# Differential and latent attention of layer 0 emitted side by side

## The chip, the cores and the metric

One Trainium2 chip, one core. The metric is device time of one execution in microseconds; lower is better. All data are float32; TensorE (PE) multiplies mostly in the float32r format, and a value that needs more precision is carried as a pair "hi" (rounded) and "lo" (the rest).

## What is computed

A trunk of two layers on x (1024 tokens by 1024). Layer 0 has two groups of attention heads beside each other: eight heads of latent attention ("DSA": each query sees the 256 keys that an indexer picked, as a mask here) and four differential heads (two softmax maps each). Their outputs are concatenated and go through one output projection. Cut to layer 0:

```python
def dsa_attention(...):      # 8 heads of 64; s = q_lat.c * scale + bias over the selected keys
    p = softmax(s); return p @ c_sel @ w_uv
def diff_attention(...):     # 4 heads, two maps of 64 each, values of 128
    p = softmax(q.k * scale + bias, causal in chunks of 64)      # (head, map)
    a = p[:, :, 0] - lam * p[:, :, 1]
    return rms_norm(a @ v, b_subln) * (1.0 - lam_init)
def even_mixer(...):
    return concatenate([o_a, o_b], -1) @ w_out
x = x + rms_norm(y, g[1])    # then memory cross-attention, MLP; layer 1 alike with windowed attention
```

## The kernel before

The program is written once, unrolled, in `Net`. `even` (L355) is layer 0's mixer: input projections and the indexer; `topk_steps`, which turns the tile `score` into the tile `mask` with scratch tiles `tk_gt`, `tk_eq`, `tk_w`; the attention; `out_proj`.

Attention works in blocks of 128 queries (eight per head) against all earlier keys. `diff_unit` (L698) is one block of a differential head; `dsa_unit` (L779) one block of a latent head. A unit has steps: `load` (first unit of a head only: a bias tile `H` of 512 KB, the query and key tiles `att_q`, `att_kh`, `att_kl` of 512 KB each per map by `load_qk`, the values `v` of 512 KB, all issued on SP); `probs` (scores on PE into a PSUM bank of tag S, L312 and for the mask L315; bias and row maximum on VectorE (DVE), L329; exponential on ScalarE (ACT), L331; normalising or joining the two maps on GpSimd (POOL)); `flip` (128x128 transposes on PE into a bank of tag T, L255, and copies or hi/lo splits out of it); `pv` (probabilities times values, L743 for differential, L812 for latent heads, one for two blocks); for differential heads also `norm`, `scale`, `back`.

`pipeline` (L40) emits the steps with lags [2, 1, 1, 1, 1, 1]: in L400 all 32 differential units come first and then all 64 latent ones. Emission order is a priority, not the final order: the framework simulates the program with its own times for instructions and transfers, and each engine gets a fixed order out of that simulation, which it then runs strictly in order, waiting on semaphores. PSUM has four banks of tag S and four of tag T.

SBUF is laid out as a stack: pools lie one behind the other in the order in which they are opened (L395 to L399), in the space that the stage before left, and a tile may be written once the old tiles under it have had their last reader. Per partition, behind `mask`, the stage before has `score` at 0 to 16.5 KB, `tk_gt` at 71 to 73, `tk_eq` at 73 to 75 and `tk_w` at 75 to 79 KB, and from 88 KB on the weight tiles (from the other end of SBUF). The attention of before puts six score tiles `s` at 0 to 24 KB, the two `H` at 24 to 32, and, after a filler `gap`, `att_q` from 88 KB on.

Head outputs are stored as hi/lo pairs in `oT` (L773, L774 for differential heads; L817 through `split`, L129 and L130, for latent ones, out of a tile `os`); `out_proj` (L855) uses them as they are. Its eight weights come by `load_w` (L113): a raw tile (two of them), hi on ACT (L120), lo on DVE (L122) or POOL (L125).

Of the kernel before, what the change touches and what calls it, by code (L numbers as in the profile page):

```python
# [12 lines left out]
F32 = mybir.dt.float32  # L13
# [55 lines left out]
class Net:  # L69
# [222 lines left out]
    def load_bias(self, h, pool):  # L292
        nc = self.nc
        H = pool.tile([P, 1024], F32, name="H", bufs=2)
# [23 lines left out]

    def softmax_raw(self, Q, K, H, i, sp, bufs, mask=None):
# [12 lines left out]
        return s, sm  # L332

    def pt_tiles(self, w, pool):
        nc = self.nc
        nk = 2 * w + 2
        out = []
        for c in range((nk + 3) // 4):
            out.append((pool.tile([P, 4, 256], F32R, name="pt_hi", bufs=3),
                        pool.tile([P, 4, 256], F32R, name="pt_lo", bufs=3)))  # L340
# [14 lines left out]
    def even(self):  # L355
        nc, A = self.nc, self.A
        z = {}
        with ExitStack() as sp_:
            with ExitStack() as st:
# [44 lines left out]
            act = self.out_proj(oT, W, A["ev_out"], 1, 2, self.x_in, x1)  # L404
        return act, x1

# [239 lines left out]
    def load_qk(self, zq, zk, j, pool):  # L646
        nc = self.nc
        rows = slice(64 * j, 64 * j + 64)
        q = pool.tile([P, S], F32R, name="att_q")
        kh = pool.tile([P, S], F32R, name="att_kh")  # L650
        kl = pool.tile([P, S], F32R, name="att_kl")
# [34 lines left out]
    def dsa_units(self, z, oT, mask, offs, R):  # L686
        units = []
        for p in range(4):
            pair = {}
            for j in range(2):  # L690
                hd = {}
                for w in range(4):
                    win = {}
                    for b in range(2):
                        units.append(self.dsa_unit(p, j, w, b, hd, win, pair, z, oT, R, mask, offs))
        return units

    def diff_unit(self, h, w, b, hd, win, z, oT, R, nlam, gsub):  # L698
# [4 lines left out]
        def load():  # L703
            hd["H"] = self.load_bias(8 + h, R)
            hd["maps"] = [self.load_qk(z["qb"][h], z["kb"][h], m, R) for m in range(2)]
            hd["V"] = R.tile([P, NT, P], F32, name="v", bufs=4)
            nc.sync.dma_start(hd["V"], z["vb"][:, :, h * P:(h + 1) * P].rearrange("t p d -> p t d"))

        def probs():
# [4 lines left out]
            (s0, m0), (s1, m1) = (self.softmax_raw(q, k, hd["H"], blk, R, 6) for q, k in hd["maps"])  # L714
# [11 lines left out]
        def flip():  # L726
            if b == 0:
                win["pt"] = [R.tile([P, 4, 256], F32, name=("pt_hi", "pt_lo")[c % 2], bufs=3) for c in range(w // 2 + 1)]
# [39 lines left out]
        def back():  # L768
# [10 lines left out]
    def dsa_unit(self, p, j, w, b, hd, win, pair, z, oT, R, mask, offs):  # L779
        nc = self.nc  # L780
        blk = 2 * w + b
        h = 2 * p + j
        n = P * (blk + 1)
        u = {}

        def load():
            hd["H"] = self.load_bias(h, R)
            hd["q"], hd["k"] = self.load_qk(z["qa"][p], z["ka"][p], j, R)
# [3 lines left out]
        def probs():  # L792
            mk = mask[:, offs[blk]:offs[blk] + n] if blk >= BLK0 else None
            s, m = self.softmax_raw(hd["q"], hd["k"], hd["H"], blk, R, 6, mk)
            r = self.small(name="ra")
            nc.vector.reciprocal(r, m)
            nc.gpsimd.tensor_scalar(s[:, 0:n], s[:, 0:n], r, 1.0, op0=ALU.mult, op1=ALU.mult)
            u["s"] = s

        def flip():  # L800
            if b == 0:
                win["pt"] = self.pt_tiles(w, R)
            self.pt_fill(win["pt"], u["s"], blk)

        def pv():
            if j == 0 and w == 0:
                pair["os"] = R.tile([P, S], F32, name="os", bufs=2)
            po = self.ps("o")
            nk = 2 * w + 2
            for kt in range(nk):  # L810
                for x in range(2):
                    nc.tensor.matmul(po[:, 0:256], lhsT=hd["v"][:, kt], rhs=win["pt"][kt // 4][x][:, kt % 4],  # L812
                                     start=kt == 0 and x == 0, stop=kt == nk - 1 and x == 1)
# [5 lines left out]
        return [load if w == 0 and b == 0 else None, probs, flip] + ([pv] if b == 1 else [])  # L819
# [9 lines left out]
    def out_unit(self, t, oT, W, g1, g2, x_src, x_dst, nat, act, to_mlp=False):  # L829
# [13 lines left out]
        def flip():  # L843
# [5 lines left out]
            if t % 4 == 0:  # L849
                act.append(self.act_pair())  # L850
# [4 lines left out]
    def out_proj(self, oT, W, rows, i1, i2, x_src, x_dst):  # L855
        nc, A = self.nc, self.A
        with ExitStack() as st:
# [6 lines left out]
            act = []  # L864

            def lhs(t):
                a = oT[t // 4]
# [3 lines left out]
            pipeline([self.out_unit(t, lhs, W, g1, g2, x_src, x_dst, R, act) for t in range(NT)], [2])  # L871
# [707 lines left out]
```

## Time and profile before

| | us |
|---|---|
| three runs, median (lowest to highest) | 2575.03 (2570.91 to 2583.68) |
| the profiled execution's own time | 2570.29 |
| its span, first to last instruction | 2568.5 |
| TensorE busy in the span | 2415.0 (94%) |
| VectorE, ScalarE, GpSimd busy | 1705.3, 1424.4, 725.4 |

Times of day below are microseconds from the span's start. The attention of layer 0 runs from about 362 to 647. A busy PE counts a matmul with its drain, so two neighbours overlap; the step from one start to the next is the price in a dense stream.

### The profile page before, as it was taken

How to read it: one execution, taken by the hardware profiler on the slowest of the kernel's cores; microseconds unless marked ns; L12 is line 12 of the kernel's file. 1: busy time of each engine (PE TensorE's matmuls, PEld its weight loads, DVE VectorE, ACT ScalarE, POOL GpSimd, SP SyncE). 2: the span in 40 equal slices, each digit the busy share in tenths (PEclk: the TensorE clock that was granted, in tenths of full speed). 3: DMA queues.
4: the chain of work that ended last, by engine and by line, in shares of the span. 5: the costliest groups of instructions: out<-in, count | busy, mean ns of one | idle time of the engine just before them, and what ended most of it. 6: DMA issues, size and time to landing. Idle time of an engine off the chain costs nothing. (4 is left out here: it accounts for less than half of the span.)

```text
span 2568.5 us, 34640 instructions
## 1 busy us (share of the span) xinstructions
PE 2415.0 (94%) x11478; PEld 1975.6 (77%) x11493; DVE 1705.3 (66%) x3240; ACT 1424.4 (55%) x2820; POOL 725.4 (28%) x1262
## 2 busy tenths in 40 slices
PE   7999988899998989999999999989988899999997
PEld 6877867778877767887888888868776688788886
DVE  5699676698458765655665878864686656556556
ACT  5577747688347544554443568863574445534433
POOL 5322125545333111112111444441421122211113
PEclk9999989899999999999999999999999999999999
DMA  5226365664424444458776521132245434678665
GB/s 180 87 84 219 130 195 132 142 159 111 152 99 160 160 154 145 160 195 295 256 251 208 184 103 38 38 114 104 98 160 181 151 140 158 236 253 272 221 220 173
DMA packets 157473, 418.53 MB, mean 163 GB/s; under 512 B 21050, under 2 KB 39406, under 8 KB 157294
## 3 DMA queue, kind: packets, MB, share of 16 engines
q1 hardware_dynamic: 119982, 287.32, 34.9%
q0 software_dynamic: 37312, 129.00, 14.0%
q8 instruction: 91, 1.49, 0.2%
q14 instruction: 88, 0.72, 0.1%
HBM read 296.05 MB, written 120.19 MB: 162 GB/s over the span
## 5 line engine op out<-in xcount | busy, mean ns | idle before, releaser
L129 ACT ACTIVATE l_hi<-l_raw 128x1024 fp32r<-128x1024 f32 x112 | 118.5, 1060 | 303.1 <-PE ps_T L1287 135.7
L1117 POOL DMA_DIRECT2D dr<-ua x192 | 103.6, 540 | 470.6 <-ACT ua L1114 335.0
L125 POOL TENSOR_TENSOR w_lo<-w_raw,w_hi 128x512 fp32r<-128x512 f32 x118 | 161.2, 1390 | 237.5 <-ACT w_hi L120 224.7
L130 DVE TENSOR_TENSOR l_lo<-l_raw,l_hi 128x1024 fp32r<-128x1024 f32 x112 | 136.7, 1223 | 135.1 <-ACT l_hi L129 133.6
L140 PE MATMUL ps_S<-act_hi,w_hi 128*128 128x512 f32 x512 | 201.9, 396 | 2.5 <-DVE z_lo L130 1.2
L141 PE MATMUL ps_S<-act_lo,w_hi 128*128 128x512 f32 x512 | 200.5, 392 | 2.3 <-DVE act_lo L130 2.3
L142 PE MATMUL ps_S<-act_hi,w_lo 128*128 128x512 f32 x512 | 199.5, 390 | 0.2 <-POOL w_lo L125 0.2
L1287 PE MATMUL ps_S<-w_hi,l_hi 128*128 128x512 f32 x480 | 188.3, 394 | 1.4 <-ACT l_hi L129 1.4
L1287 PE MATMUL ps_S<-w_hi,l_lo 128*128 128x512 f32 x480 | 187.8, 393 | 0.6 <-DVE l_lo L130 0.6
L1287 PE MATMUL ps_S<-w_lo,l_hi 128*128 128x512 f32 x480 | 186.8, 389 | 0.0
L1238 POOL DMA_DIRECT2D l_raw<-dr x112 | 60.7, 542 | 378.7 <-DVE l_lo L130 367.1
L129 ACT ACTIVATE s_hi<-w_raw 128x512 fp32r<-128x512 f32 x160 | 99.8, 628 | 84.8 <-PE ps_S L1106 37.6
L140 PE MATMUL ps_S<-w_hi,act_hi 128*128 128x512 f32 x320 | 125.5, 400 | 4.0 <-DVE yn L195 3.7
L141 PE MATMUL ps_S<-w_lo,act_hi 128*128 128x512 f32 x320 | 126.5, 396 | 1.3 <-DVE w_lo L122 1.1
L142 PE MATMUL ps_S<-w_hi,act_lo 128*128 128x512 f32 x320 | 126.0, 394 | 0.0
L130 DVE TENSOR_TENSOR s_lo<-w_raw,s_hi 128x512 fp32r<-128x512 f32 x160 | 108.8, 686 | 21.0 <-ACT s_hi L129 20.4
L140 PEld LDWEIGHTS ps_S<-act_hi,w_hi 128*128 128x128 f32 x512 | 96.2, 188 | 24.7 <-DVE onm L1449 2.3
L1113 ACT ACTIVATE ua<-ua 128x512 f32<-128x512 f32 x76 | 47.8, 629 | 120.0 <-DVE ua L1160 77.2
L1106 PE MATMUL ps_S<-t_h,s_hi 128*128 128x512 f32 x256 | 103.7, 406 | 10.7 <-ACT s_hi L129 10.6
L141 PEld LDWEIGHTS ps_S<-act_lo,w_hi 128*128 128x128 f32 x512 | 96.2, 188 | 21.6 <-DVE act_lo L130 3.1
L142 PEld LDWEIGHTS ps_S<-act_hi,w_lo 128*128 128x128 f32 x512 | 96.1, 188 | 19.9 <-POOL w_lo L125 0.6
L331 ACT ACTIVATE s<-s,nm 128x128 f32<-128x128 f32 (+7 forms) x128 | 99.1, 778 | 19.3 <-DVE nm L329 18.8
(376 smaller groups left out, 7403.7 us busy)
## 6 DMA issues: line engine op xcount, KB each, us to landing
l_raw<-dr POOLq DMA_DIRECT2D x112, 512.0 KB, 4.2
dr<-ua POOLq DMA_DIRECT2D x204, 256.0 KB, 2.7
w_raw<-w SPq DMA_DIRECT2D x76, 512.0 KB, 3.7
w_lo<-w SPq DMA_DIRECT2D x128, 256.0 KB, 4.3
w_hi<-w SPq DMA_DIRECT2D x128, 256.0 KB, 4.6
x_dram<-xt SPq DMA_DIRECT2D x40, 512.0 KB, 3.1
xt<-x_dram SPq DMA_DIRECT2D x40, 512.0 KB, 3.5
w_raw<-ev_fm SPq DMA_DIRECT2D x18, 512.0 KB, 4.1
```

What stands on the lines that cost most here:

```text
L125: nc.gpsimd.tensor_tensor(lo[:, cs], raw[:, cs], hi[:, cs].bitcast(F32), ALU.subtract)
L129: self.nc.scalar.activation(hi, src, AF.Copy)
L130: self.nc.vector.tensor_tensor(lo, src, hi.bitcast(F32), ALU.subtract)
L140: nc.tensor.matmul(ps, lhsT=a[0], rhs=b[0], start=first, stop=False)
L141: nc.tensor.matmul(ps, lhsT=a[0], rhs=b[1], start=False, stop=False)
L142: nc.tensor.matmul(ps, lhsT=a[1], rhs=b[0], start=False, stop=last)
L331: nc.scalar.activation(s[:, 0:n], s[:, 0:n], AF.Exp, bias=nm, scale=-1.0, accum_out=sm)
L1106: nc.tensor.matmul(ps, lhsT=w[i], rhs=B[b][j][:, k], start=first and k == 0 and n == 0, stop=k == 3 and n == 2, skip_group_check=True)
L1113: nc.scalar.activation(c, c, AF.Relu)
L1117: nc.gpsimd.dma_start(left[i][p // 2][:, p % 2], c)
L1238: nc.gpsimd.dma_start(a, left[i][b])
L1287: nc.tensor.matmul(banks[z][t], lhsT=x[i], rhs=w[j][:, e], start=start and b == 0 and e == 0 and n == 0, stop=b == NB - 1 and e == 1 and n ...
```

## The change

The four differential heads (32 units) and the eight latent heads (now 32 units of two blocks each, a window) are emitted in one loop, the latent ones two steps behind; within a step, `pv` comes before `flip`. Each kind has its own rings for `att_*` tiles (three for differential, two for latent), its own bias ring (`Hd` one tile, `Hs` two) and its own transposed tiles (`pt` for differential). The score tiles leave the rings: eight of them (`exps`) lie in the two `act_lo` buffers, taken in turn. Head outputs are written once, unsplit, into two tiles in the `act_hi` buffers; `out_proj` splits the 128 columns that it needs, up to three blocks ahead, into `o_hi` and `o_lo`. The filler `gap` and the tile `os` are gone.

```diff
-                oT = [self.act_pair(), self.act_pair()]
+                oT = [self.actp.tile([P, KD, 512], F32, name="o_%d" % x, tag="act_hi") for x in range(2)]
+                room = [self.actp.tile([P, KD // 2, 1024], F32, name="exp_%d" % x, tag="act_lo") for x in range(2)]
+                self.exps = [t[:, k] for t in room for k in range(KD // 2)]
...
-                    R.open(("s", 6), ("H", 2), ("v", 4), ("ot", 2), ("on", 2), ("os", 2), ("fold", 2), ("pt_hi", 3), ("pt_lo", 3))
-                    self.pool(s1, "gap").tile([P, 528], F32, name="gap")
-                    R.open(("att_q", 3))
-                    R.open(("att_kh", 3), ("att_kl", 3), first=1)
-                    pipeline(self.diff_units(z, oT, R) + self.dsa_units(z, oT, mask, offs, R), [2, 1, 1, 1, 1, 1])
+                    R.open(("Hd", 1), ("Hs", 2), ("v", 4), ("ot", 2), ("on", 2), ("fold", 2), ("pt_hi", 3), ("pt_lo", 3), ("pt", 2))
+                    R.open(*((x + k, n) for k, n in (("d", 3), ("s", 2)) for x in ("att_q", "att_kh", "att_kl")))
+                    self.attention(self.diff_units(z, oT, R), self.dsa_units(z, oT, mask, offs, R))
...
+        SHIFT = 2
+        n = max(len(diff), len(dsa) + SHIFT)
+        for step in range(n + 8):
+            for k in (0, 1, 3, 2, 4, 5, 6):
+                for units, shift in ((diff, 0), (dsa, SHIFT)):
+                    i = step - shift - (0 if k == 0 else k + 1)
+                    if 0 <= i < len(units) and k < len(units[i]) and units[i][k] is not None:
+                        units[i][k]()
...
-        s = sp.tile([P, 1024], F32, name="s", bufs=bufs)
+        s = self.exps[self.exp_n % len(self.exps)]
+        self.exp_n += 1
...
-            hi, lo = a[0][:, 4 + h, c0:c0 + 256], a[1][:, 4 + h, c0:c0 + 256]
-            nc.scalar.activation(hi, pt2[:, 0:256], AF.Copy, scale=gsub)
-            nc.vector.scalar_tensor_tensor(lo, pt2[:, 0:256], gsub, hi.bitcast(F32), ALU.mult, ALU.subtract)
+            nc.scalar.activation(a[:, 4 + h, c0:c0 + 256], pt2[:, 0:256], AF.Copy, scale=gsub)
...
         def probs():
+            for b in range(2):
+                blk = 2 * w + b
...
-            self.fold(pair["os"][64 * j:64 * j + 64, w * 256:w * 256 + 256], po[:, 0:256], R)
-            if j == 1 and w % 2 == 1:
-                a = oT[w // 2]
-                self.split(a[0][:, p], a[1][:, p], pair["os"][:, (w // 2) * 512:(w // 2) * 512 + 512])
+            c0 = (w % 2) * 256
+            self.fold(oT[w // 2][64 * j:64 * j + 64, p, c0:c0 + 256], po[:, 0:256], R)
...
+            def lhs_raw(t):
+                for x in range(t, min(t + 3, NT)):
+                    if x not in split:
+                        hi, lo = (R.tile([P, KD, P], F32R, name="o" + n, bufs=3) for n in ("_hi", "_lo"))
+                        self.split(hi, lo, oT[x // 4][:, :, (x % 4) * P:(x % 4) * P + P])
+                        split[x] = hi, lo
```

## Rows read from the trace of the kernel before

**Rows 1.** The page: granted TensorE clock, tenths of full speed, in 40 slices.
```profile
PEclk9999989899999999999999999999999999999999
```
**Rows 2.** Windows: us from:to, length, then busy us per engine, clock, DMA.
```profile
372.00:392.00 20.00, 16.79 (x66) 13.68 (x67) 14.38 (x59) 12.10 (x36) 12.62 (x22) 0.72 0.30 80
392.00:505.00 113.00, 94.48 (x498) 80.05 (x498) 76.58 (x276) 80.54 (x242) 65.36 (x131) 0.90 0.62 145
505.00:624.00 119.00, 115.98 (x785) 94.86 (x799) 106.37 (x350) 99.39 (x243) 55.47 (x124) 1.00 0.56 134
624.00:650.00 26.00, 26.00 (x151) 22.50 (x150) 14.45 (x27) 14.11 (x26) 12.92 (x14) 1.00 0.40 131
650.00:745.00 95.00, 94.73 (x444) 76.81 (x443) 43.91 (x53) 35.48 (x76) 24.50 (x40) 1.00 0.43 150
520.00:620.00 100.00, 97.78 (x675) 80.80 (x685) 92.61 (x305) 85.12 (x206) 47.62 (x108) 1.00 0.56 132
```
**Rows 3.** The same view where one differential head gives way to the next.
```profile
490.00:500.00 10.00, 6.18 (x38) 4.95 (x36) 4.12 (x16) 4.28 (x15) 3.21 (x10) 0.96 0.99 235
```
**Rows 4.** Timeline of PE in dense stretches: start, length, line, tiles, count.
```profile
478.02 0.40 PE L312 MATMUL ps_S<-att_kh,att_q 128*128 128x512 f32 x1
478.26 0.40 PE L312 MATMUL ps_S<-att_kl,att_q 128*128 128x512 f32 x1
...
565.78 0.28 PE L812 MATMUL ps_T<-pt_lo,v 128*128 128x256 f32 x1
565.90 0.60 PE L255 MATMUL ps_T<-ident,s 128*128 128x128 f32 x4
566.26 0.48 PE L312 MATMUL ps_S<-att_kh,att_q 128*128 128x512 f32 x1
...
389.61 1.89 PE L743 MATMUL ps_T<-pt_hi,v 128*128 128x256 f32 x8
391.15 0.58 PE L312 MATMUL ps_S<-att_kh,att_q 128*128 128x512 f32 x1
```
**Rows 5.** Groups by form on PE, 505 to 650: the output projection's part.
```profile
L142 PE MATMUL ps_S<-w_hi,act_lo 128*128 128x512 f32 x25 | 9.9, 397 | 0.0
```
**Rows 6.** Groups on DVE, 372 to 650: the lo halves of head outputs.
```profile
L774 DVE SCALAR_TENSOR_TENSOR act_lo<-ps_T,gsub,act_hi 128x256 fp32r<-128x256 f32 x16 | 7.6, 475 | 0.6 <-ACT act_hi L773 0.6
L130 DVE TENSOR_TENSOR act_lo<-os,act_hi 128x512 fp32r<-128x512 f32 x8 | 6.9, 868 | 0.7 <-ACT act_hi L129 0.7
```
**Rows 7.** The page's groups: a split of 128x1024, its DVE half.
```profile
L130 DVE TENSOR_TENSOR l_lo<-l_raw,l_hi 128x1024 fp32r<-128x1024 f32 x112 | 136.7, 1223 | 135.1 <-ACT l_hi L129 133.6
```
**Rows 8.** Timeline of DVE at the start; then tile `H`, its DMAs' time to landing.
```profile
370.24 1.25 DVE L547 TENSOR_SCALAR_CACHE_REDUCE tk_gt<-score,tk_thr 128x1024 bf16<-128x1024 f32 x1
372.08 0.28 DVE L329 CUSTOM_DVE_ANT_0 s<-ps_S,H 128x128 f32<-128x128 f32 x1
372.84 1.28 DVE L551 SCALAR_TENSOR_TENSOR tk_eq<-tk_w,tk_need,tk_eq 128x1024 bf16<-128x1024 f32 x1
...
DMA to landing us min/median/max: 6.9/8.3/10.1
```
**Rows 9.** Waits between 362 and 512, PE and POOL; then SP's own, 355 to 650.
```profile
PE ps_S L312 <- DMA att_kh<-dr: 9.7, 3, 4.3
POOL H L296 <- DMA H<-dr: 11.4, 4, 6.0
...
SPq L790 <- PE ps_T L743: 49.1, 4, 14.8
```
**Rows 10.** Timelines at the end: PE's last scores; SP's first output weight, four later.
```profile
621.47 0.39 PE L312 MATMUL ps_S<-att_kl,att_q 128*128 128x512 f32 x1
...
517.20 0.35 SPq L117 DMA_DIRECT2D w_raw<-ev_out  x1
626.64 12.86 SPq L117 DMA_DIRECT2D w_raw<-ev_out  x4
```
**Rows 11.** DMA issues, 355 to 660: the output weights, count, KB, us to landing.
```profile
w_raw<-ev_out SPq DMA_DIRECT2D x8, 512.0 KB, 3.7
```

More of the change, by code (lines that the diff above doesn't have):

```diff
@@ L338, in pt_tiles @@
         for c in range((nk + 3) // 4):
-            out.append((pool.tile([P, 4, 256], F32R, name="pt_hi", bufs=3),
-                        pool.tile([P, 4, 256], F32R, name="pt_lo", bufs=3)))
+            out.append((pool.tile([P, 4, 256], F32R, name="pt_hi"),
+                        pool.tile([P, 4, 256], F32R, name="pt_lo")))
         k = nk - 1
@@ L403, in even, with attention @@
             x1 = self.x_dram()
[L404 removed]
+            act = self.out_proj(oT, W, A["ev_out"], 1, 2, self.x_in, x1, True)
         return act, x1
+    @staticmethod
+    def attention(diff, dsa):
+        SHIFT = 2
[6 more added lines that the diff above has]
+                        units[i][k]()
     def indexer(self, act, ip, mp, score, offs):
@@ L644, in even_rest, with load_qk @@
         pump(100, 100)
-    def load_qk(self, zq, zk, j, pool):
+    def load_qk(self, zq, zk, j, pool, kind):
         nc = self.nc
         rows = slice(64 * j, 64 * j + 64)
-        q = pool.tile([P, S], F32R, name="att_q")
-        kh = pool.tile([P, S], F32R, name="att_kh")
-        kl = pool.tile([P, S], F32R, name="att_kl")
+        q = pool.tile([P, S], F32R, name="att_q" + kind)
+        kh = pool.tile([P, S], F32R, name="att_kh" + kind)
+        kl = pool.tile([P, S], F32R, name="att_kl" + kind)
         nc.sync.dma_start(q[0:64].bitcast(F32), zq[0][rows])
@@ L692, in dsa_units @@
                 for w in range(4):
-                    win = {}
-                    for b in range(2):
-                        units.append(self.dsa_unit(p, j, w, b, hd, win, pair, z, oT, R, mask, offs))
+                    units.append(self.dsa_unit(p, j, w, hd, z, oT, R, mask, offs))
         return units
@@ L703, in load @@
         def load():
-            hd["H"] = self.load_bias(8 + h, R)
-            hd["maps"] = [self.load_qk(z["qb"][h], z["kb"][h], m, R) for m in range(2)]
+            hd["H"] = self.load_bias(8 + h, R, "Hd")
+            hd["maps"] = [self.load_qk(z["qb"][h], z["kb"][h], m, R, "d") for m in range(2)]
             hd["V"] = R.tile([P, NT, P], F32, name="v", bufs=4)
@@ L713, in probs @@
             n = P * (blk + 1)
-            (s0, m0), (s1, m1) = (self.softmax_raw(q, k, hd["H"], blk, R, 6) for q, k in hd["maps"])
+            (s0, m0), (s1, m1) = (self.softmax_raw(q, k, hd["H"], blk) for q, k in hd["maps"])
             cc = self.small(name="cc")
@@ L727, in flip @@
             if b == 0:
-                win["pt"] = [R.tile([P, 4, 256], F32, name=("pt_hi", "pt_lo")[c % 2], bufs=3) for c in range(w // 2 + 1)]
+                win["pt"] = [R.tile([P, 4, 256], F32, name="pt") for c in range(w // 2 + 1)]
                 k = 2 * w + 1
@@ L792, in probs @@
         def probs():
[L793 to L798, printed above, removed]
+            for b in range(2):
+                blk = 2 * w + b
+                n = P * (blk + 1)
+                mk = mask[:, offs[blk]:offs[blk] + n] if blk >= BLK0 else None
+                s, m = self.softmax_raw(hd["q"], hd["k"], hd["H"], blk, mk)
+                r = self.small(name="ra")
+                nc.vector.reciprocal(r, m)
+                nc.gpsimd.tensor_scalar(s[:, 0:n], s[:, 0:n], r, 1.0, op0=ALU.mult, op1=ALU.mult)
+                u["s"].append(s)
         def flip():
-            if b == 0:
-                win["pt"] = self.pt_tiles(w, R)
-            self.pt_fill(win["pt"], u["s"], blk)
+            u["pt"] = self.pt_tiles(w, R)
+            for b in range(2):
+                self.pt_fill(u["pt"], u["s"][b], 2 * w + b)
         def pv():
-            if j == 0 and w == 0:
-                pair["os"] = R.tile([P, S], F32, name="os", bufs=2)
             po = self.ps("o")
@@ L811, in pv @@
                 for x in range(2):
[L812 removed]
+                    nc.tensor.matmul(po[:, 0:256], lhsT=hd["v"][:, kt], rhs=u["pt"][kt // 4][x][:, kt % 4],
                                      start=kt == 0 and x == 0, stop=kt == nk - 1 and x == 1)
[L814 to L819 removed]
+            c0 = (w % 2) * 256
+            self.fold(oT[w // 2][64 * j:64 * j + 64, p, c0:c0 + 256], po[:, 0:256], R)
+        return [load if w == 0 else None, probs, flip, pv]
     def fold(self, dst, po, pool):
@@ L849, in flip, with out_proj @@
             if t % 4 == 0:
-                act.append(self.act_pair())
+                act.append(self.act_pair() if pair is None else pair(t // 4))
             self.pre_b(u["h"], act[t // 4], (t % 4) * P)
         return [mm, flip]
-    def out_proj(self, oT, W, rows, i1, i2, x_src, x_dst):
+    def out_proj(self, oT, W, rows, i1, i2, x_src, x_dst, raw=False):
         nc, A = self.nc, self.A
@@ L864, in out_proj @@
             act = []
+            split = {}
+            def lhs_raw(t):
[4 more added lines that the diff above has]
+                        split[x] = hi, lo
+                a = split[t]
+                return lambda k: (a[0][:, k], a[1][:, k])
             def lhs(t):
+                if raw:
+                    return lhs_raw(t)
                 a = oT[t // 4]
@@ L869, in lhs @@
                 return lambda k: (a[0][:, k, sl], a[1][:, k, sl])
-            pipeline([self.out_unit(t, lhs, W, g1, g2, x_src, x_dst, R, act) for t in range(NT)], [2])
+            pair = None
+            if raw:
+                pair = lambda half: tuple(self.actp.tile([P, KD, 512], F32R, name="act_" + n, tag=("act_lo", "act_hi")[half])
+                                          for n in ("hi", "lo"))
+            pipeline([self.out_unit(t, lhs, W, g1, g2, x_src, x_dst, R, act, pair=pair) for t in range(NT)], [2])
         return act
```

20 lines of the change are left out of this document (9 added, 11 removed).

## The prediction

> **What bounds the kernel now.** I read the clock row of the page first, then windows over the attention of layer 0, then the groups and timelines in it. The clock is full nearly everywhere, but dips in the slices around 360 to 510 [rows 1]: a stage where PE does not have enough to do. The windows [rows 2] show two regimes. While the differential heads run (372 to 505) no engine is full: PE is busy 111.3 of 133 us at a granted clock of 0.72 and then 0.90, so part of that is work at 1.2 instead of 2.4 GHz, and DVE is busy 91 and ACT 92.6. The latent heads (505 to 624) are another kernel: PE 97%, DVE 89%, ACT 84%, clock 1.00. Then PE stays full through the end of the attention, into which the scheduler has already drawn output-projection matmuls, and through that projection. So PE sets the end from 505 on, and up to 505 nobody does: there it is a chain of short steps, plus a gap where one head gives way to the next, in which PE falls to about 60% and DMA is at 0.99 [rows 3]; there are four such gaps, three of them between differential heads.
>
> I therefore count the stage on PE: the work that PE must do, plus the time in which it has none.
>
> **Before, on this count.** Attention proper starts when DVE takes its first score tile at 372.1 [rows 8]. At 650 PE is saturated and has done 77 matmuls of the output projection (one row of 25 is shown, the others have 25 and 27 [rows 5]); at 94.73 us for 444 [rows 2] they are worth 16.5 us. So the attention costs 650 - 372.1 - 16.5 = 261.4 us of PE's time. This is what the change can shorten; all other stages keep their instructions.
>
> **The work of the two streams.** Latent heads: PE is busy 116 + 26 us from 505 to 650 [rows 2], less 16.5 for the projection and some 3 for the last differential steps, and plus about 5 for the eight pairs of scores that were issued before 505: 127.5 us, 15.9 per head. In a dense stretch the steps are 0.24 us for a score matmul of 512 columns, 0.12 for one of `pv`, 0.09 for a transpose, and 0.19 for a `pv` matmul of a differential head [rows 4]. A latent head has per map 9728 score columns (19 steps of 512: 4.5 us), a mask of 4224 columns (2 us), 36 transposes (3.3) and 40 `pv` matmuls (4.8): 14.6 us. So a head costs 1.09 of its dense price, for the changes from one kind of matmul to another. A differential head has two maps (9.1), 36 + 16 transposes (4.7) and 20 `pv` matmuls of 0.19 (3.9): 17.7 us dense, 19.3 at 1.09, 77 for four. From below it is 71 (dense); from above it is what PE was busy, 111.3 less 5 for the early latent scores and less some 14 for the two slow-clock windows, 92. I take 77, since the mixed stage will look like the latent one: the sum is 204.5, between 187 (both dense) and 220.
>
> DVE needs 211.8 us over 372 to 650 [rows 2] less 14.5 for the lo halves of head outputs that fall away here [rows 6] and some 6 for the end of the top-k and three weights: 191. ACT: 206 less 5 for the matching hi halves and 7 for weights: 194. The best joint rate that the trace shows is 520 to 620: PE 97.8%, DVE 92.6%, ACT 85% [rows 2]. At PE's 97.8% the mixed stage takes 209 us, in which DVE is at 91% and ACT at 93%; ACT has not been seen that full, but DVE has, so I let PE set it. Transfers: a differential head loads 4 MB and a latent one 2.5, 37.7 million bytes in all; at the 235 GB/s of the fullest slice [rows 3] they take 160 of the 209 us: no bound, if they are asked for early.
>
> **What the change adds.**
>
> (a) The start. `Hd` and `Hs` now lie first in the ring, at 0 to 12 KB, over `score` (0 to 16.5); before, the score tiles lay there and `H` at 24 KB was loaded long before. The last reader of `score` is the DVE instruction that ends at 371.5 [rows 8]. A bias tile takes 6.9 to 10.1 us from issue to landing, 8.3 in the middle [rows 8]; it then needs a short memset. So DVE's first score tile moves from 372.1 to about 380.5. The second map's `att_q` (70 to 74 KB) lies over `tk_gt` and `tk_eq`, and the first `att_kh` (78 KB) over the end of `tk_w`, whose readers end at 374 and a little later [rows 8]; they land in the same time, at about 381. Queued behind the waiting DMA on SP are the next loads, and behind the memset POOL's first steps. Price 8.4 us; from 5 (the top-k tail, now undisturbed, ends sooner) to 12.
>
> (b) The gaps between differential heads stay. Two maps of four need the slots that the head before still reads, and with one `Hd` the bias can be asked for only after the head's last score. PE waited 9.7 us in three such places [rows 9], though `H` was there. I take 10; from 0 (the other stream fills them) to 36 (rival 2).
>
> (c) The end. The first output weights used to be on the chip early (the first raw tile was asked for at 517, four after 626 [rows 10]). Now the two raw tiles lie over the latent heads' last `att_kl` tiles and the differential heads' `gsub`, so the chain of raw load (3.7 us [rows 11]), hi on ACT and lo on DVE or POOL (some 1.2 each [rows 7]) starts only after the last scores and the last `back`, and two raw buffers let two weights pass per 6 us. Before, PE had 25 us of backlog after its last score at 621.5 [rows 10]; now both streams end together, with 6 to 8 us. The projection can use each weight for two blocks (2.6 us) as it comes. That leaves PE about 9 us idle; from 3 to 18.
>
> (d) The projection splits what it needs itself: eight splits of 128x1024, 1.2 us on DVE [rows 7] and 1.1 on ACT. Both are under half busy there, from 650 to 745 [rows 2], and the split runs three blocks ahead: nothing. Without that cover each would cost some 2.3 us, 18 in all. The first of them stands with the weights in (c). `o_hi` and `o_lo` cover the space of the cross-attention's first tiles, whose loads so start later, behind its 20 us of query projection: nothing.
>
> Sum: 8.4 + 209 + 10 + 9 = 236.4 us against 261.4: 25 us less. The profiled execution took 2570.3, so 2545.3; that execution lies 4.7 under the median, and I predict 2546.
>
> **Rivals.**
>
> 1. *The streams fill each other's gaps.* The two kinds have different score tiles, rings and bias tiles, and the exps are taken four per step, so that latent units never wait for a differential unit's tile; while a differential head waits for its data, latent units alone can keep PE at 98% [rows 2]. Then (b) is 0 and (c) about 4: 221.4, 40 less, 2531. Against it: the order is fixed by simulated times, and it is the real time of the transfers that decides. The Trainium skill's page "Perfetto Trace Analysis" ("Identifying the Most-Contended Engine") would judge PE by the share of weight loads rather than of matmuls; that is 81% from 520 to 620, which would leave PE a fifth to spare; but it is also 81% in the dense projection [rows 2], so the trace does not bear it out.
>
> 2. *A convoy: same time.* Each engine runs its fixed order, so an instruction of the differential stream that waits for `Hd` holds the latent stream behind it on DVE and POOL. In before POOL stood waiting for `H` 11.4 us in four places [rows 9], so the simulation took these transfers as shorter than they are. If both streams stop for a whole bias transfer with what precedes it on the queue, 12 us at each of three changes, (b) is 36: 262.4, one us slower than before, 2572. It decides if the differential scores stand early in DVE's order, ahead of latent ones. The Trainium skill's "PSUM — Partial Sum Buffer" ("Engine vs sequencer instructions") calls the queues of ACT, DVE and POOL strict FIFOs; the rows on POOL agree.
>
> 3. *Slower: SP's queue starves the latent heads.* All loads are issued by SP in order, and one that waits for its slot holds the others: in before a `v` load stood 49.1 us in four places, up to 14.8 [rows 9]. If a latent head's loads stand behind a differential one's that waits, they come late by up to 9 us, of which the other stream covers a third: 6 for each of seven heads, 42 on top of the forecast, 278.4: 17 slower, 2588. It is slower than before from 3.6 us per head on. Against it: latent rings are double, so a head's loads have a whole head's time, over 25 us.
>
> **How the numbers follow.** Chances: forecast 0.45 (2546, its own range 2533 to 2558), rival 1 0.18, rival 2 0.20, rival 3 0.17. Runs of this kernel differ by up to 0.5%, about what a measurement can tell from no change, so over 0.5% is over 13 us. Faster: 0.42 of the forecast, all of rival 1: 0.60. Same: rival 2 and the slow end of the forecast: 0.23. Slower: 0.17. The range takes in the lowest sum (PE's work dense, 187 us, so that ACT sets the pace and does its 194 us in 204; (a) 5, (b) 0, (c) 3: 212, about 2521) and reaches to rival 3 at 2588; what it leaves out is faster than the one or slower than the other.
>
> **What would show it.** Right: DVE's first L329 at about 380 instead of 372; full clock in the slices of the attention; `pv` of both kinds (L743's and L812's successors) in the same 10 us windows; PE above 95% between 390 and 590; last fold near 605 instead of 647; a stretch there in which PE waits for output weights. Rival 2 would show as DVE and PE idle together for 10 us after a `Hd` load; rival 3 as latent scores that wait for `att_khs`. Wrong altogether: a mixed stage in which PE is below 90% with no transfer in flight, that is, where tags S or T of PSUM (four banks each, now for two streams) hold it.

## The result, and the profile after

| | us |
|---|---|
| before, median of four runs (lowest to highest) | 2572.98 (2570.91 to 2583.68) |
| after, median of four runs | 2613.54 (2612.77 to 2616.34) |
| after to before, with its 95% interval | 1.0151 (1.0121 to 1.0181) |
| the profiled execution's span, before and after | 2568.5 and 2611.9 |

The change made the kernel 1.5% slower, some 40 us, where 25 us less was forecast. The loss lies between the end of the input projections and layer 0's output projection. The same windows as in [rows 2], now of the changed kernel (us from:to, length, then busy us with instructions of PE, its weight loads, DVE, ACT and POOL; granted clock, DMA share, GB/s):

```profile
372.00:392.00 20.00, 2.52 (x10) 2.29 (x11) 6.34 (x16) 1.04 (x5) 1.88 (x6) 0.50 0.87 230
392.00:505.00 113.00, 97.05 (x553) 78.30 (x559) 81.20 (x293) 80.21 (x218) 58.33 (x118) 0.93 0.63 147
505.00:624.00 119.00, 109.38 (x673) 89.78 (x681) 87.77 (x319) 89.32 (x245) 63.49 (x132) 0.96 0.40 95
624.00:650.00 26.00, 23.20 (x142) 18.47 (x143) 20.71 (x58) 21.54 (x51) 13.95 (x25) 1.00 0.07 21
650.00:745.00 95.00, 79.70 (x358) 65.35 (x359) 38.90 (x45) 35.09 (x67) 26.99 (x36) 0.91 0.37 129
520.00:620.00 100.00, 90.59 (x552) 73.76 (x558) 74.04 (x264) 75.99 (x208) 53.77 (x110) 0.95 0.42 99
```

PE did 2.5 us of work in the first 20 us, where it had done 16.8; from 505 to 624 it was 92% busy instead of 97%; from 650 to 745 it lost 15 us to idleness. Cut where PE stops, the same view shows dense stretches with holes between them:

```profile
387.00:416.00 29.00, 25.72 (x141) 21.00 (x142) 22.10 (x93) 21.93 (x61) 19.72 (x33) 0.86 0.52 122
416.00:440.00 24.00, 17.41 (x92) 13.88 (x93) 12.67 (x39) 11.28 (x31) 6.45 (x19) 0.86 0.88 213
440.00:486.00 46.00, 44.27 (x277) 36.23 (x280) 37.93 (x143) 39.62 (x110) 27.46 (x53) 1.00 0.44 110
486.00:508.00 22.00, 14.90 (x80) 11.91 (x80) 10.14 (x28) 8.53 (x24) 5.28 (x16) 0.84 0.93 203
508.00:558.00 50.00, 48.06 (x306) 39.47 (x308) 40.79 (x152) 42.22 (x115) 30.77 (x64) 1.00 0.49 119
558.00:582.00 24.00, 18.07 (x95) 14.26 (x96) 13.02 (x49) 12.03 (x34) 6.20 (x17) 0.79 0.44 105
582.00:640.00 58.00, 55.89 (x353) 46.07 (x357) 47.33 (x163) 47.40 (x128) 32.28 (x66) 1.00 0.20 47
640.00:662.00 22.00, 15.47 (x89) 12.80 (x87) 12.09 (x24) 14.94 (x34) 12.63 (x15) 0.92 0.19 58
662.00:682.00 20.00, 9.98 (x31) 7.83 (x32) 1.64 (x2) 5.44 (x8) 7.50 (x6) 0.66 0.63 226
```

The three long stretches at clock 1.00 (PE 96%, DVE 82% and ACT 84% over the three) are the side-by-side stage as forecast. The holes are a late start (until 387), one stop at each of the three changes of differential head (in 416 to 440, 486 to 508, 558 to 582: 6.6, 7.1 and 5.9 us without PE) and the end (640 to 682: 16.5 us). Each hole also costs through the clock: the granted mean falls below 1.00, part of the stretch at 1.2 instead of 2.4 GHz, each time after PE has idled. By the same column before lost clock too: 0.72 over the first 20 us and 0.90 over the next 113 [rows 2].

**The start.** DVE, then SP, then PE:

```profile
373.17 1.25 DVE L564 TENSOR_SCALAR_CACHE_REDUCE tk_gt<-score,tk_thr 128x1024 bf16<-128x1024 f32 x1
387.63 0.29 DVE L330 CUSTOM_DVE_ANT_0 exp<-ps_S,Hd 128x128 f32<-128x128 f32 x1 [10.49 <-PE ps_S L312]
```
```profile
374.45 0.33 SPq L295 DMA_DIRECT2D Hd<-dr  x1
375.43 0.42 SPq L721 DMA_DIRECT2D v<-dr  x1
375.91 1.77 SPq L295 DMA_DIRECT2D Hs<-dr  x1
377.78 0.47 SPq L672 DMA_DIRECT2D att_khd<-dr  x1
378.94 0.59 SPq L673 DMA_DIRECT2D att_khs<-dr  x1
```
```profile
386.73 0.55 PE L312 MATMUL ps_S<-att_khd,att_qd 128*128 128x256 f32 x1 [20.42 <-DMA att_khs<-dr]
390.24 0.55 PE L312 MATMUL ps_S<-att_khd,att_qd 128*128 128x256 f32 x1 [2.75 <-DMA att_qd<-dr]
```

SP waits for the last reader of `score` (DVE L564, until 374.4) with `Hd`. `Hd` itself lands in 4.1 us, sooner than I had it. But `att_khd` stands behind it on SP, is issued at 377.8 and shares the transfer engines with `v`, `Hs` and `att_khs`: PE's first score comes at 386.7, and the second map's, which waits for its `att_qd`, at 390.2. (The first PE row names `att_khs`, a latent load under way at the same time; the score itself reads `att_khd` and `att_qd`.) The last reader of `score` also ended 2.9 us later than in before, 374.4 for 371.5. So DVE's first score is 15.5 us later than in [rows 8].

**A stop**, here the first: SP's first and last load of the keys that PE waits for, and `Hd`; then PE, then DVE.

```profile
416.97 0.44 SPq L672 DMA_DIRECT2D att_khd<-dr  x1
...
422.53 0.77 SPq L673 DMA_DIRECT2D att_kld<-dr  x1
...
430.29 0.33 SPq L295 DMA_DIRECT2D Hd<-dr  x1
```
```profile
424.91 0.47 PE L312 MATMUL ps_S<-att_khd,att_qd 128*128 128x256 f32 x1
...
429.32 0.55 PE L312 MATMUL ps_S<-att_khd,att_qd 128*128 128x256 f32 x1 [2.58 <-DVE pt_lo L130]
431.41 0.55 PE L312 MATMUL ps_S<-att_kld,att_qd 128*128 128x256 f32 x1 [1.54 <-DMA att_kld<-dr]
431.76 4.92 PE L757 MATMUL ps_T<-pt,v 128*128 128x256 f32 x12
436.33 0.58 PE L312 MATMUL ps_S<-att_khs,att_qs 128*128 128x512 f32 x1
```
```profile
431.33 0.15 DVE L809 RECIPROCAL ra<-sum 128x1 f32<-128x1 f32 x1
436.72 0.42 DVE L760 COPY ot<-ps_T 128x256 f32<-128x256 f32 x1 [5.24 <-PE ps_T L757]
439.90 0.29 DVE L330 CUSTOM_DVE_ANT_0 exp<-ps_S,Hd 128x128 f32<-128x128 f32 x1 [2.75 <-PE ps_T L255]
```

The new head's first scores stand on PE ahead of the latent stream's (436.33) and wait for their key tiles. Late are the tiles of its second map only: the first map's lie in the third slot, and its score ran at 424.91 without a wait. The second map's take the slot of the old head's first map; SP asks for them at 416.97, as that map's last score runs (PE, 416.78), so its queue doesn't hold them up further. They come behind the loads of a latent head (issued from 411.90 to 415.44), with DMA at 0.88, and PE gets them at 429.32 and 431.41. (The row puts the first of these waits down to DVE; at the other two stops the same wait, 3.9 and 4.2 us, is put down to `att_khd`.) The two waits are 4.1 of the 6.6 us without PE; 2.4 came just before, for POOL. Meanwhile DVE has nothing to read for 5.2 us (6.7 and 7.7 at the other two stops), until the twelve `pv` matmuls behind these scores are done. Those take 4.57 us to the start of the next line, 0.38 each, twice the 0.19 of [rows 4] counted in the same way.

### The profile page after: what moved, and what is told of

Its sections match the earlier page's. It is cut to its first block, busy times and chain, and to the rows that moved or that the text cites. A ratio compares the mean times of both kernels' runs of the same rounds, so it can differ in the third digit from the quotient of the medians.

```text
span 2611.9 us, 34472 instructions
## 1 busy us (share of the span) xinstructions
PE 2424.5 (93%) x11474; PEld 1981.6 (76%) x11493; DVE 1701.3 (65%) x3224; ACT 1426.2 (55%) x2820; POOL 727.9 (28%) x1262
## 5 line engine op out<-in xcount | busy, mean ns | idle before, releaser
L125 POOL TENSOR_TENSOR w_lo<-w_raw,w_hi 128x512 fp32r<-128x512 f32 x118 | 157.7, 1360 | 263.2 <-ACT w_hi L120 252.0
L130 DVE TENSOR_TENSOR s_lo<-w_raw,s_hi 128x512 fp32r<-128x512 f32 x160 | 108.6, 686 | 21.5 <-ACT s_hi L129 20.9
L332 ACT ACTIVATE exp<-exp,nm 128x896 f32<-128x896 f32 (+7 forms) x128 | 98.7, 775 | 34.2 <-DVE nm L330 32.9
L120 ACT ACTIVATE w_hi<-w_raw 128x1024 fp32r<-128x1024 f32 x65 | 68.3, 1056 | 77.3 <-PE ps_S L141 25.2
L1313 PEld LDWEIGHTS ps_S<-w_hi,l_lo 128*128 128x128 f32 x480 | 90.0, 188 | 22.0 <-DVE l_lo L130 1.1
L1313 PEld LDWEIGHTS ps_S<-w_hi,l_hi 128*128 128x128 f32 x480 | 90.2, 188 | 20.4 <-ACT l_hi L129 1.8
```

The costliest lines, as they stand in the source:

```text
L120: nc.scalar.activation(hi, raw, AF.Copy)
L125: nc.gpsimd.tensor_tensor(lo[:, cs], raw[:, cs], hi[:, cs].bitcast(F32), ALU.subtract)
L130: self.nc.vector.tensor_tensor(lo, src, hi.bitcast(F32), ALU.subtract)
L1313: nc.tensor.matmul(banks[z][t], lhsT=x[i], rhs=w[j][:, e], start=start and b == 0 and e == 0 and n == 0, stop=b == NB - 1 and e == 1 and n ...
```

## The experiments

The changed kernel's lines are meant unless said otherwise. Times are medians; "before" was run beside each group, and its medians were 2572.2 to 2574.2.

**1. The start alone.** The ring slots are opened one by one in another order (`place` takes them from the lowest address up), so that nothing needed early lies over `score` or the top-k's scratch:

```diff
-                    R.open(("Hd", 1), ("Hs", 2), ("v", 4), ("ot", 2), ("on", 2), ("fold", 2), ("pt_hi", 3), ("pt_lo", 3), ("pt", 2))
-                    R.open(*((x + k, n) for k, n in (("d", 3), ("s", 2)) for x in ("att_q", "att_kh", "att_kl")))
+                    R.place(
+                            ("pt_hi", 0), ("pt_hi", 1), ("pt_hi", 2), ("pt_lo", 0), ("pt_lo", 1), ("pt_lo", 2),
+                            ("Hd", 0), ("Hs", 0), ("Hs", 1), ("ot", 0), ("ot", 1), ("on", 0),
+                            ("on", 1), ("fold", 0), ("fold", 1), ("pt", 0), ("pt", 1), ("att_qd", 2),
+                            ("v", 0), ("v", 1), ("v", 2), ("v", 3), ("att_khd", 2), ("att_kld", 2),
+                            ("att_qs", 1), ("att_qd", 0), ("att_qd", 1), ("att_khd", 0), ("att_khd", 1), ("att_kld", 0),
+                            ("att_kld", 1), ("att_qs", 0), ("att_khs", 0), ("att_khs", 1), ("att_kls", 0), ("att_kls", 1))
```

> Only the order of the attention's ring slots changes: Hd, Hs, v and the first head's q and k lie over space that has been free for a while; the split probabilities, which are needed some 20 us later, lie over score; the third d slots and the second latent q lie over the top-k's last tiles. Theory (the late start comes from tiles that must wait for the top-k's last readers): DVE's first differential score moves from 387.6 back to 376 or earlier, and the whole time falls by about 11 us (some 2602). Rival (the first loads are late because seven tiles load at once on busy DMA queues, wherever they lie): the first score stays after 383 and the time falls by under 5 us.

Measured: 2598.8, 14.7 less. DVE's first score (in this kernel L335 is that line) stands 13 us earlier:

```profile
374.62 0.28 DVE L335 CUSTOM_DVE_ANT_0 exp<-ps_S,Hd 128x128 f32<-128x128 f32 x1
```

So the place of the tiles made the start late; the crowd of transfers follows from it and isn't a cause by itself.

**2 to 4. What stops both streams at a head change.** Heads 1 to 3 keep head 0's bias, its maps' tiles, or both (the edits of the three runs in one, shortened):

```diff
-            hd["H"] = self.load_bias(8 + h, R, "Hd")
+            if h == 0: self.kept = {"H": self.load_bias(8, R, "Hd")}
+            hd["H"] = self.kept["H"]                  # runs 2 and 4
-            hd["maps"] = [self.load_qk(z["qb"][h], z["kb"][h], m, R, "d") for m in range(2)]
+            if h == 0: self.kept["maps"] = [self.load_qk(z["qb"][0], z["kb"][0], m, R, "d") for m in range(2)]
+            hd["maps"] = self.kept["maps"]            # runs 3 and 4
```

> Heads 1 to 3 of the differential stream keep head 0's bias tile Hd (their own bias is left out), all else as in the changed kernel. Theory (the three stops between differential heads come from the one Hd, which can be asked for only after the head's last score, with both streams queued in order behind it): DVE's and PE's stops at 430, 497 and 570 go, 5 to 7 us each, and the time falls by 15 to 20 us (some 2596). Rival (the q and k loads that stand ahead of Hd on SP's queue and wait for their slots are what comes late): the stops stay at half or more and the time falls by under 7 us.

> Heads 1 to 3 of the differential stream keep head 0's q and k tiles of both maps (the right maps of heads 1 to 3 are left out), but each still loads its own bias Hd. Keeping Hd alone brought nothing, keeping both brought 26 us. Theory (the two maps' 3 MB and their place ahead of Hd on SP's queue are the whole stop; Hd alone, asked for in time, comes unnoticed): as with both kept, some 2588. Rival (each of the two is enough to stop both streams, the load of Hd after the head's last score as well): three stops of 4 to 6 us stay, some 2600 to 2610.

> Heads 1 to 3 of the differential stream keep head 0's Hd and both its maps' q and k tiles (the right scores of heads 1 to 3 are left out); only v is loaded. Theory (the stops between heads are waits for loads and for nothing else): all three go, PE stays at full clock from 400 to 640, and the time falls by 20 us, to some 2593. If a third or more of the stops stays, the streams' own dependencies make them: the time then falls by under 12 us.

Measured: bias kept 2614.2, maps kept 2586.6, both kept 2587.2. The three stretches of the stops with the bias kept, and then with the maps kept:

```profile
416.00:440.00 24.00, 17.80 (x90) 13.89 (x90) 13.24 (x39) 11.63 (x31) 7.01 (x18) 0.86 0.86 197
486.00:508.00 22.00, 15.55 (x91) 12.80 (x91) 11.76 (x36) 10.28 (x31) 6.96 (x17) 0.84 0.85 184
558.00:582.00 24.00, 18.34 (x102) 14.34 (x103) 14.59 (x51) 13.12 (x37) 6.64 (x18) 0.86 0.35 81
```
```profile
416.00:440.00 24.00, 21.67 (x139) 17.53 (x137) 19.54 (x70) 17.76 (x50) 9.79 (x26) 1.00 0.47 119
486.00:508.00 22.00, 21.68 (x136) 17.97 (x135) 16.55 (x60) 16.45 (x47) 11.54 (x27) 1.00 0.37 99
558.00:582.00 24.00, 23.14 (x151) 19.41 (x150) 17.28 (x61) 19.08 (x57) 15.57 (x35) 1.00 0.48 111
```

My theory that the single `Hd` sets the stop fell: without its loads nothing changes. The query and key tiles are the cause: without their loads PE's holes shrink to 2.3, 0.3 and 0.9 us, the clock stays full, and 27 us go, more than the 19.6 us of idleness. The rest is, by the clock column, work that no longer runs at the lower clock; no run shows it apart.

**5. Side by side undone, all else kept:**

```diff
-        SHIFT = 2
+        SHIFT = len(diff)
```

> Only the emission is undone: the changed kernel's tiles, rings and output projection, but all differential units ahead of all latent units. Forecast's theory (with the differential heads alone PE has about 25 us of room that the latent stream fills): 20 to 30 us slower than the changed kernel, some 2638. Rival (PE's own work, with the differential v matmuls recorded twice each, was 17 us larger than I counted, so that there was little room to fill, and the stops at head changes now halt both streams): within 10 us of the changed kernel, either side.

Measured: 2602.2, 11 us faster than the changed kernel, just outside the rival's band and far from the forecast's theory. With these rings, running the streams together is itself a loss.

**6. The disputed price, differential `pv`.**

```diff
-            for kt in range(2 * w + 2):
-                nc.tensor.matmul(po[:, 0:256], lhsT=hd["V"][:, kt], rhs=win["pt"][kt // 4][:, kt % 4], start=kt == 0,
-                                 stop=kt == 2 * w + 1)
+            nc.tensor.matmul(po[:, 0:256], lhsT=hd["V"][:, 0], rhs=win["pt"][0][:, 0], start=True, stop=True)
```

> The differential heads' product with v is cut to its first key block (16 instructions of 80 stay in all four heads; the rest of the sum over key blocks is left out). It measures the disputed term of the sum by itself. If a differential head's v product is 20 matmuls of 0.19 us, as I counted, 64 fewer are 12 us of PE; if each of them is two, as the 160 records of the trace say, they are 24 us. As PE is the bound in the mixed stretches only and idles at the head changes, up to a third may be lost there: 2613 less 8 to 12 us by my count (2601 to 2605), less 16 to 26 us by the records (2587 to 2597).

Measured: 2596.7, 16.8 less: in the band of the records, outside that of my count. The groups of that matmul on PE from 362 to 690, first of the changed kernel (80 instructions), then of this one (16):

```profile
L757 PE MATMUL ps_T<-pt,v 128*128 128x256 f32 x160 | 44.4, 433 | 1.3 <-DVE pt_lo L130 1.1
```
```profile
L756 PE MATMUL ps_T<-pt,v 128*128 128x256 f32 x32 | 11.0, 427 | 1.6 <-DVE pt_lo L130 1.5
```

Each instruction is two records, and the second is paid for: 16.8 us is more than 64 instructions of 0.19 us could give (12.2). It is less than 128 records would (24.3); what kept the rest from showing isn't separated, and the mean clock was also a little lower, 0.968 for 0.971. So a head has 40 records, 7.6 us by the 0.19 of my sum, not 20 and 3.9. The 0.19 is itself a little low. The lowest, median and highest time of one record in before, in ns:

```profile
L743 PE MATMUL ps_T<-pt_hi,v x112: 377/379/634, 382.7 to 504.3; 128*128 128x256 f32 x112
```

With 0.38 for the last of them, the eight records of [rows 4] (1.89 us) start 0.216 us apart; the 0.19 came from counting to the start of the next line. The factor 1.09 makes up for most of it.

**7 and 8. Filling the stops.** The differential stream pauses for two steps at each head change and asks for its loads at the start of the pause:

```diff
+        paced = []
+        for i, unit in enumerate(diff):
+            if i and i % 8 == 0:
+                paced += [[unit[0]]] + [[]]
+                unit = [None] + unit[1:]
+            paced.append(unit)
+        diff = paced
```

First with the ring order of run 1 (7), then with the changed kernel's own rings (8).

> The first experiment's ring order, and in the emission the differential stream pauses for two steps at each of its three head changes, while its next loads are asked for at the start of the pause; the latent stream goes on, so that two latent units stand ahead of the new head's first scores in every engine's order. Theory (a stop costs both streams only because the differential scores that wait stand ahead of latent ones on DVE and PE): most of the three stops is filled, 12 to 18 us off the first experiment's 2598.8, some 2584. Rival (the stops come from SP's queue and from rings that hold up the latent stream's own loads too, or what is saved comes back as a longer stretch with the differential stream alone at the end): within 5 us of 2599.

> The changed kernel with its own rings and the two-step pauses of the differential stream at its head changes, nothing else. With the mended start the pauses brought 20.7 us (2598.8 to 2578.1). If start and stops are separate losses they bring the same here: 2613.5 less 20, some 2593. If the late start shifts the loads so that the pauses miss them, or the stops here have another cause, under 12 us: over 2601.

Measured: 2578.1 and 2589.0, so 20.7 and 24.5 less than without the pauses, more than I expected. The work and the loads are the same; only the order differs, and the differential stream's end, six steps later. So the stop costs both streams because the waiting scores stand ahead of the latent ones. From 380 to 610 PE is now 95% busy in run 7, at nearly full clock:

```profile
380.00:610.00 230.00, 218.78 (x1386) 180.08 (x1385) 189.07 (x665) 189.29 (x506) 132.30 (x267) 0.99 0.54 131
```

**9. Side by side undone with the start mended** (runs 1 and 5 together):

> The first experiment's ring order with all differential units ahead of all latent units: what side by side is worth when the start is mended. By the sums so far, undoing the interleaving brought 11 us with the original rings (2602 against 2613.5). If the stops of both streams at the three head changes are the cost of side by side, and the start is a separate cost, the same holds here: 2598.8 less 11, some 2588, and the kernel with pauses (2578) is then 10 us under it, which is what side by side brings once it doesn't stop. If the start's crowding was part of the interleaving's loss (a second stream loading at once), this comes out within 4 us of 2598.8.

Measured: 2583.1, 15.8 under run 1, although its own first score came 3.8 us later. The six kernels make a table:

| | own rings | start mended |
|---|---|---|
| side by side, as the change has it | 2613.5 | 2598.8 |
| one stream after the other | 2602.2 | 2583.1 |
| side by side with pauses | 2589.0 | 2578.1 |

The mended start brings 14.7, 19.1 and 10.9 us in the three rows, so the two losses add, though only roughly. Side by side is worth 5 to 13 us against one after the other once it doesn't stop; as emitted it costs 11 to 16. The 5 is barely clear of noise: the two kernels' times to before are 1.0004 to 1.0025 and 1.0020 to 1.0043.

**10 to 12. The end.** The latent stream runs eight steps behind (10, 11) or twelve (12), and the slots are placed so that the output projection's first weights lie over differential tiles and the norm's tiles below them; 11 and 12 also give four weights two raw buffers of their own, and split head outputs up to two blocks ahead instead of three (pauses, slot order and the smaller split rings aren't shown):

```diff
-        SHIFT = 2
+        SHIFT = 8
...
+            W = W + [self.load_w(rows[k], nc.vector if k % 2 == 0 else None, R, nw, R if raw and k % 4 >= 2 else None) for k in range(len(W), KD)]
```

> As the kernel with pauses, with the latent stream eight steps behind instead of two, so that it ends alone some four steps after the differential one, and with the slots placed so that the output projection's first weights lie over differential tiles, the norm's tiles below them over what is freed last. Theory (the stretch from 640 to 682, in which PE waits for weights, is the third loss): its idle time falls by 10 to 15 us, but the first differential head runs without cover, which costs about 5: some 8 under the kernel with pauses, near 2576. If the weights come no sooner, or the uncovered first head costs as much: within 4 us of the kernel with pauses.

> As the fourth-last kernel's plan (pauses, latent stream eight steps behind, the first output weights over early tiles), with the raw tiles of output weights 2, 3, 6 and 7 in two buffers of their own, so that four raw tiles instead of two are under way, and the norm's x tiles over v slots. Theory (after the attention PE waits, some 10 us from 620 to 632, for a chain of raw load, hi and lo that two raw buffers make serial): half of that wait or more goes, 5 to 8 us under that kernel's 2571.3, some 2565. Rival (the wait is for the first of the weights, which SP's queue holds behind other waiting loads): within 3 us of 2571.

> The same with the latent stream twelve steps behind, so that more of the differential tiles are free before the end, while the first differential head and a half run alone. Theory (the room at the end is worth more than cover for the first differential heads): 0 to 5 us under the kernel with eight steps. Rival (a differential head alone leaves PE some 7 us idle, as in the kernel before): 3 to 7 us over it.

Measured: run 10 2571.3, to before 0.9998 (0.9989 to 1.0007); run 11 2575.4, to before 0.9998 (0.9987 to 1.0009); run 12 2585.4, to before 1.0039 (1.0024 to 1.0055). Run 10 is the whole loss recovered, but no gain. More raw buffers bring nothing: PE is busy 38.9 of 50 us from 610 to 660 in run 10 and 38.3 in run 11, so that my account of the last hole (two raw buffers in series) fell, as far as the smaller split rings of run 11 let one compare. Twelve steps cost some 10 us against run 11, the rival's side and more than its 3 to 7. Windows of run 10, then of before:

```profile
380.00:610.00 230.00, 215.46 (x1344) 175.81 (x1344) 182.66 (x644) 183.02 (x493) 127.49 (x264) 0.99 0.57 135
610.00:660.00 50.00, 38.94 (x184) 30.05 (x183) 17.61 (x22) 22.41 (x40) 19.08 (x20) 0.93 0.36 120
```
```profile
380.00:610.00 230.00, 207.59 (x1238) 173.09 (x1252) 178.52 (x617) 173.78 (x471) 119.00 (x251) 0.93 0.58 136
610.00:660.00 50.00, 49.27 (x280) 40.43 (x281) 29.78 (x72) 31.38 (x65) 26.43 (x35) 1.00 0.40 129
```

The best side-by-side order leaves PE 8 us less idle through the attention, at a fuller clock, and 10 us more idle behind it. The traces show what PE waits for there. In run 10, ACT's last `back`, SP's next weights, ACT's hi half, PE (L803, L122, L125 and L145 are `back`, `load_w` and `out_proj` in this kernel):

```profile
625.22 0.47 ACT L803 ACTIVATE o<-ps_T,gsub 128x256 f32<-128x256 f32 x1
625.72 13.55 SPq L122 DMA_DIRECT2D w_raw<-ev_out  x5
629.36 1.06 ACT L125 ACTIVATE w_hi<-w_raw 128x1024 fp32r<-128x1024 f32 x1 [3.67 <-DMA w_raw<-ev_out]
630.46 2.08 PE L145 MATMUL ps_S<-w_hi,o_hi 128*128 128x512 f32 x4 [7.19 <-ACT w_hi L125]
```

SP had stood 4.1 us for that `back`, the last reader of `gsub`, over which a raw tile lies by the prediction's layout. Run 11 has the same steps: the last `back` at 623.73, a weight asked for behind it, and PE idle for 9.4 us until 630.27. By these rows more raw buffers had little to shorten, since one weight is still asked for only after the last `back`. No run moved `gsub`, so this is read from the traces and not tested.

## Why the prediction was wrong

Four terms of the sum were too small, and none of them is the whole miss: the work, the start, the stops and the end. The balance below has their shares.

**The work: a count that was half of the true one.** The first step that failed is "20 `pv` matmuls of 0.19 (3.9)". Two of the rows I rested on show it: eight records for one `pv` of four key blocks, in 1.5 us [rows 4]; I took their count for the count of instructions, and it is twice that. Run 6 showed that the second record is paid for. A head is then 21.5 us dense, 23.4 at my 1.09, 94 for four; with 127.5 for the latent heads 221, and 226 instead of 209 at 97.8%. My own sum would have come to 253.4, 8 us less than before: 2562, inside the half per cent. The room that the change was to fill was smaller than I had it: PE's idle time from 372 to 650 in before is 24.8 us [rows 2], and its busy time there, 253.2, is 15.7 more than the corrected work (221 and 16.5), mostly the lower clock's. That is 40 us for everything. I promised 25 of them after paying 27 for (a), (b) and (c); the two don't go together, and setting the sum beside the idle time would have told me.

**(a) The start: 15.5 for 8.4, outside 5 to 12.** The place and the reader were right. I priced one transfer, and that was even shorter (4.1 us). The reader ended 2.9 us later where I had it end sooner. What was late behind the transfer I had in view, "the next loads", and set them to land in the same time; they queue on SP behind `Hd` and land after it, the first keys at 386.7, the second map's queries at 390.2. Run 1 brings 14.7.

**(b) The stops: 10 for some 25, between my ends of 0 and 36.** This is rival 2 in its form: in every engine's order the differential stream's waiting instruction stands ahead of the latent stream's, and both halt. It isn't rival 2 in its cause: I named `Hd`, DVE and POOL; it is the query and key tiles, and PE (runs 2 and 3). I had the row, 9.7 us of PE waiting for `att_kh` in three such places [rows 9], and took it as the price. That is what it cost when one stream waited: the step that failed is the overlap, a wait of one stream that I let cost no more with two. The page "PSUM — Partial Sum Buffer" of the Trainium skill ("Engine vs sequencer instructions") also says that matmuls start and finish in program order; the trace agrees, for the latent score at 436.33 did not pass the differential one at 431.41. I had cited that section for the other three queues alone. The sign I gave, DVE and PE idle together for 10 us after a `Hd` load, showed in weaker form: DVE idle 5.2, 6.7 and 7.7 us.

**(c) The end: 9, from 3 to 18; PE's idleness was 16.5 us, at a clock of 0.92 and 0.66.** The mechanism was as told: SP's first output weight waits for the last latent score, and PE for a weight. SP's wait and PE's:

```profile
SPq L117 <- PE ps_S L315: 45.3, 1, 45.3
PE ps_S L140 <- ACT w_hi L120: 9.5, 1, 9.5
```

PE's wait is for a later weight than the first, the one behind the last `back`, as I had it in (c): that `back` runs at 663.18, SP asks for the weight at 663.68, and its hi half is done at 672.56, just before PE starts at 672.61. From asking to landing it took 7.8 us where I had 3.7, with four loads of the norm just ahead of it on SP. The size stayed inside my range for idleness alone. Runs 10 and 11 show the same wait with the first weights asked for earlier.

**What no term had: the clock.** I put stops down as idle time at full clock. Around each hole PE works at 1.2 GHz for a while: the stretches from 387 to 440, 486 to 508, 558 to 582 and 640 to 682 have granted means of 0.86, 0.86, 0.84, 0.79, 0.92 and 0.66. One minus the mean, times the length, is 24.5 us in all: an upper estimate, as part of it fell on idle time. By the same count before lost 16.9 us, from 372 to 505 [rows 2]; my 77 for the differential work handed all of that back.

**The balance.** In my own count PE has done 64 output matmuls by 690 (22, 21 and 21 of the three products; at the 0.213 us of [rows 2] they are 13.7 us), so the stage cost 690 - 372.1 - 13.7 = 304.2 us against 261.4: 42.8 more, which agrees with the spans' 43.4. Of it, 226 are the work and 15.5 the start; the pauses take away 24.5 (run 8); about 38 are left for the end, the start's slow clock and the small holes in between, against 9 in my sum. The stage came out 67.8 us over my 236.4: the work is 17 of that, the start 7, the stops 14.5 and what is left 29, of which PE's idleness at the end is 7.5 and the rest no run separates. From the other side: start 14.7 (run 1), pauses 20.7 (run 7), the end 6.8 (run 10, with its later latent stream and other places): 42.2; before lies 40.6 below the change.

**The other rivals and (d).** Rival 1, gaps filled by the other stream, is what the pauses make of the kernel; by itself the emission doesn't do it. Rival 3 did not come: the one long wait that the profile puts down to `att_khs` is at the start, and there it is a differential score's. The range (2520 to 2588) let one thing go wrong at a time. The upper ends together (12, 36 and 18 us on 209) give 275, or 2584; with the right count of `pv` 292, or 2601. The 12 us from there to the measured time are, I think, the clock's; no run shows them apart. A late start, stops and an empty end are not independent: all follow from both streams taking up and giving back their tiles at the same moments. The price of zero for the splits of (d) was not tried by itself.

## What to carry to other kernels

Before forecasting what an overlap brings, take the bounding engine's idle time in the stage, and what its lower clock costs there: together they are the ceiling, and a sum of work that promises more has a wrong count in it. Two streams in one emission share every queue, so that a wait costs both; where one stream must reload, let it pause in the emission and put the other's work ahead of it. And a stage whose last part is one dense stream may be worth its place: behind its latent heads the kernel before had its weights on the chip and 25 us of PE's work in hand.

## What the runs showed of the hardware

- A plain float32 matmul of 256 columns (`pt`, `v`) is two records that start 0.216 us apart in a dense stretch, 0.43 us per instruction, where the float32r one of the same shape takes 0.12.
- The same 512 KB bias tile landed in 4.1 to 7.1 us (`Hd`) and in 6.2 to 12.9 us (`Hs`); the 12.9 is among the loads that crowd at the start.
- After PE had waited 2.6 and 1.5 us, the twelve matmul records that followed took 0.38 us each where the same count gives 0.19 in a dense stretch; the three stops cost 26 to 27 us (runs 3 and 4) where PE's idleness in them was 19.6.
